# A decoder layer in split fp32 on one core: a gate stage's products put together, a reduction moved to the end of a queue, a pass's sums behind the next split, and more rooms for raw weights

## The chip, the cores and the metric

The kernel runs on one core of a Trainium2 chip. The time is device microseconds (us) of one execution; the kernel before was run three times, and the median of the three stands for it. TensorE (PE) does the matmuls, VectorE (DVE) and ScalarE (ACT) the work on elements, SyncE (SP) issues nearly all DMA loads. Each engine works through its instructions in the order of the program and stops at the first one whose inputs, or whose room, are not there yet.

## The reference

One decoder layer over 256 tokens of width 2048, all in fp32:

```python
h = rmsnorm(x, norm_mix_pre)
xr, yr, q, k, v, g_rnn, g_attn = split(h @ w_in)
xr = rg_lru(causal_depthwise_conv(xr), ...)      # block-diagonal gates: tanh/sigmoid of xb @ w_a, xb @ w_x
y_rnn = xr * gelu(yr)
y_att = sliding_window_sink_attention(rope(q), rope(k), v, sinks)
mix = sigmoid(g_rnn) * (y_rnn @ w_rnn_proj) + sigmoid(g_attn) * (y_att @ w_attn_proj)
x = x + rmsnorm(mix @ w_out, norm_mix_post)
u = square(relu(rmsnorm(x, norm_mlp_pre) @ w_mlp_up))
x = x + rmsnorm(u @ w_mlp_down, norm_mlp_post)
```

The up and down projections (2048 to 8192 and back) are over half of the weights that are read.

## The kernel before

**Products.** A number in fp32 is carried as two float32r parts, `hi` (the value cast down) and `lo` (what the cast left). A product of two such numbers is three matmuls: hi·hi, lo·hi, hi·lo. Weights arrive from memory as raw fp32 in halves of 128 x 1024 (512 KB). For each half ACT casts `whi` (L116), DVE subtracts to get `wlo` (L122), and PE uses both.

**The stream of weights.** The class `Stream` holds all weights in the order of their use. `load_to` issues SP's loads into the rooms `wraw` (four of them, `WRAW`), `split_to` emits cast and subtraction, `half` hands the next pair of parts to the matmul code and runs ahead: the split by six halves (`AHEAD`), the load by a few more. A load into a room waits until the subtraction that last read the room is done. There are six rooms each for `whi` and `wlo`. A second pool, tag `U8`, has 12 rooms of 128 x 2048 for activations and other large tiles.

**The recurrent stage.** `recur(m)` and `gates(m)` alternate for m = 0..3. `gates(m)` handles the two blocks n = 2m and 2m+1; each has two gates, and each gate is 12 matmuls of 128 x 256 into a bank `pg`, followed by two tanh on ACT (L799) that read the bank. For the odd block the two gates lie in the two banks of one pair tile. The matmuls that follow on PE belong to the next projection (`ps`, L264 with whi and L272 with wlo). Where nothing is pinned, a list scheduler with priorities sets the order on each engine; `fix` (keep_in_program_order) pins an instruction at its place.

**The residual.** After `w_out`, a generator `residual` is advanced step by step by `pump()`: for each half of the tokens (tb) and each quarter of the columns it forms the new x on DVE, squares it with a row sum on ACT, and writes x away. After the four quarters of a tb come a reduce, a root and a reciprocal (`rms`), and a diagonal matrix `dg`. `spread_r2` multiplies `ones` by both `dg` on PE (tile `pr`), which spreads the factor over all partitions; the first evacuations of the up projection need it. The pumps are spread over the opening of the up projection.

**Up and down.** The feed-forward work is done in two halves f = 0, 1: up (16 a-passes), then down in two passes n = 0, 1 of 1024 output columns each. A down pass goes over 16 pairs of weight halves. Seven of them (`SEVEN`: 0, 2, ..., 12) are done with seven products in place of eight (Strassen): DVE forms sums of the weights into a tile `t` (three operations), ACT and DVE split a, b and t (`whi`, `wlo`, `thi`, `tlo`), and PE runs 21 matmuls of 128 x 512. The other nine pairs are plain, 24 matmuls each. `t`, `thi` and `tlo` of each seven are U8 rooms. Eight banks are in use: four (`P1`, `P6` in s0, `Q5`, `N7` in s1) are complete after pair 12, four (`Q3`, `P2`, `Q4`, `Cs`) run to the end. After pair 12, DVE combines the first four into four tiles `t` (the sums; for f = 1 the earlier half's result `acc` is added too: eight DVE operations, `early`), and after the last matmul of each of the other banks, `finish` adds the bank to its tile. The last `held` pairs (2, and 3 in the very last pass) are done bank by bank, so that banks end one after another.

**Between the passes.** f = 0 writes its results to memory (`acc_away`); in f = 1 the generators `back` load them again, and in the last pass x1, the residual, as 256 KB pieces through SP, pumped between the pairs. The last pass also multiplies by a gain (`g3`), forms the row sums of squares, and ends with scale-and-add and the output's DMAs.

## Time and profile before

| | |
|---|---|
| three runs | 1540.43, 1539.72, 1537.09 us; median 1539.72 |
| the profiled execution | 1540.81 us; its span from first to last instruction 1539.0 us, so 1.8 us lie around it |
| PE busy | 1510.8 us, 98% of the span |
| DVE, ACT busy | 1108.1 us (72%), 826.4 us (54%) |
| granted PE clock, mean | 0.993 |
| HBM | 288.6 MB read, 192 GB/s over the span |

Times in the profile's rows are from the span's start. A row of a timeline has start, duration, engine, line, operation, out<-in, and in brackets how long the engine had been idle before and what released it. PEclk is the clock that PE was granted as a part of the full one, averaged over the stretch. The stages that matter here: recurrent stage with gates to about 585 us, up f0 from about 838, down f0 to 1174.7, up f1 to 1352.3, down f1 n0 to 1438.8, n1 to 1530.3, then the tail.

### The profile page before, as it was taken

The page shows a single profiled execution, that of the slowest core. Times are in us where ns is not written, and L with a number is a line of the kernel's source. Part 1 is how long each engine was busy: PE and PEld are TensorE (multiplying, and loading weights), DVE is VectorE, ACT ScalarE, POOL GpSimd, SP SyncE. Part 2 cuts the span into 40 slices and gives each one's busy share as a digit, 9 for nine tenths or more (in the row PEclk, how much of TensorE's full clock was granted, in tenths as well). Part 3 has the DMA queues.
Part 4 walks back from the last instruction along what each step waited for, and adds up shares of the span by engine and source line. Part 5 has one row for each costly group of instructions (what it writes and reads, how often), then busy time and mean ns, then how long its engine had stood idle before and what let it go on. Part 6 is the DMA issues. An engine that isn't in the chain of part 4 may idle for free.

```text
span 1539.0 us, 19994 instructions
## 1 busy us (share of the span) xinstructions
PE 1510.8 (98%) x7602; PEld 1267.5 (82%) x7602; DVE 1108.1 (72%) x1373; ACT 826.4 (54%) x1135; POOL 1.7 (0%) x9
## 2 busy tenths in 40 slices
PE   9999999999999999999999999999999999999996
PEld 7877778788888788888889888888888888888784
DVE  6676667857768867555667776689886666698877
ACT  6555555647566756444445555455454555555543
POOL 0000000000000000000000000000000000000000
PEclk9999999999999999999999999999999999999998
DMA  7645444364645565655865565656666655657574
GB/s 285 196 146 170 137 146 159 117 212 156 225 153 189 177 209 175 209 190 185 290 199 188 166 199 185 202 181 209 225 208 233 199 184 189 194 187 259 177 245 143
DMA packets 84191, 296.19 MB, mean 192 GB/s; under 512 B 9856, under 2 KB 10112, under 8 KB 83584
## 3 DMA queue, kind: packets, MB, share of 16 engines
q1 hardware_dynamic: 81072, 289.67, 57.6%
q10 hardware_dynamic: 3024, 5.25, 0.9%
q8 instruction: 59, 0.97, 0.3%
q14 instruction: 36, 0.29, 0.1%
HBM read 288.60 MB, written 6.29 MB: 192 GB/s over the span
## 4 chain that ended last, share of the span: by engine, by line
PE 83%; DVE 8%; DMA 5%; ACT 2%; issue 1%; SPq 0%; DVEq 0%; ACTq 0%
PE ps L931 20%; PE ps L264 6%; PE dQ L931 5%; DMA wraw<-in_w_dn 5%; DVE wlo L122 4%; PE ps L272 4%; PE dP L931 3%; PE s L931 2%; PE dCs L931 2%; PE gr L296 2%; PE gr L298 2%; PE pr L296 2%; PE pr L298 2%; PE pr L300 2%; PE pa L300 2%; PE pa L298 2%
## 5 line engine op out<-in xcount | busy, mean ns | idle before, releaser
L122 DVE TENSOR_TENSOR wlo<-wraw,whi 128x1024 fp32r<-128x1024 f32 x520 | 621.3, 1221 | 234.5 <-ACT whi L116 213.9
L116 ACT CAST whi<-wraw 128x1024 fp32r<-128x1024 f32 x520 | 533.5, 1050 | 461.3 <-DVE wraw L61 74.6
L931 PE MATMUL ps<-h2T,whi 128*128 128x512 f32 x976 | 228.8, 392 | 0.0
L931 PEld LDWEIGHTS ps<-h2T,whi 128*128 128x128 f32 x976 | 182.4, 189 | 36.9
L931 PEld LDWEIGHTS ps<-h2T,wlo 128*128 128x128 f32 x1024 | 127.0, 192 | 2.4
L931 PE MATMUL ps<-h2T,wlo 128*128 128x256 f32 x1024 | 127.9, 283 | 0.0
L264 PE MATMUL ps<-hT,whi 128*128 128x512 f32 x512 | 122.5, 395 | 0.0
L264 PEld LDWEIGHTS ps<-hT,whi 128*128 128x128 f32 x512 | 95.9, 190 | 20.5 <-issue 1.1
L931 PE MATMUL dQ<-whi,uT 128*128 128x512 f32 x288 | 107.8, 392 | 1.0 <-ACT whi L116 1.0
L272 PEld LDWEIGHTS ps<-hT,wlo 128*128 128x128 f32 x512 | 63.8, 191 | 1.8 <-issue 0.7
L272 PE MATMUL ps<-hT,wlo 128*128 128x256 f32 x512 | 65.2, 284 | 0.0
L931 PEld LDWEIGHTS dQ<-whi,uT 128*128 128x128 f32 x288 | 54.3, 189 | 13.1 <-ACT whi L116 2.2
L931 PE MATMUL dQ<-wlo,uT 128*128 128x512 f32 x144 | 57.0, 396 | 5.4 <-DVE wlo L122 5.4
L285 ACT COPY u<-ps 128x512 f32<-128x512 f32 x32 | 18.7, 585 | 80.2 <-PE ps L931 80.2
L61 DVE TENSOR_TENSOR t<-wraw,wraw 128x1024 f32<-128x1024 f32 x28 | 34.3, 1224 | 29.3 <-DMA wraw<-in_w_dn 28.1
L931 PE MATMUL dCs<-whi,uT 128*128 128x512 f32 x144 | 54.9, 398 | 0.0
L931 PE MATMUL dP<-whi,uT 128*128 128x512 f32 x144 | 53.8, 389 | 0.0
L296 PE MATMUL ga<-whi,hT 128*128 128x512 f32 x128 | 51.2, 400 | 0.0
L296 PE MATMUL q<-whi,hT 128*128 128x512 f32 x128 | 51.1, 399 | 0.0
L298 PE MATMUL ga<-wlo,hT 128*128 128x512 f32 x128 | 50.3, 393 | 0.0
L300 PE MATMUL ga<-whi,hT 128*128 128x512 f32 x128 | 50.2, 392 | 0.0
L298 PE MATMUL q<-wlo,hT 128*128 128x512 f32 x128 | 50.2, 392 | 0.0
(289 smaller groups left out, 2648.7 us busy)
## 6 DMA issues: line engine op xcount, KB each, us to landing
wraw<-in_w_dn SPq DMA_DIRECT2D x128, 512.0 KB, 5.0
wraw<-in_w_up SPq DMA_DIRECT2D x124, 512.0 KB, 5.0
wraw<-in_w_g SPq DMA_DIRECT2D x64, 512.0 KB, 4.7
wraw<-in_w_xy SPq DMA_DIRECT2D x64, 512.0 KB, 4.7
wraw<-in_w_q SPq DMA_DIRECT2D x32, 512.0 KB, 3.9
wraw<-in_w_ap SPq DMA_DIRECT2D x32, 512.0 KB, 4.7
wraw<-in_w_rp SPq DMA_DIRECT2D x32, 512.0 KB, 4.7
wraw<-in_w_out SPq DMA_DIRECT2D x32, 512.0 KB, 5.1
```

The source lines that it names most:

```text
L61: return lambda *args, **kw: self.pin(method(*args, **kw))
L116: self.pin(self.nc.scalar.copy(hi, src))
L122: self.last_low = self.pin(self.nc.vector.tensor_tensor(lo, src, hi.bitcast(F32), ALU.subtract))
L264: mm(ps[:, f].rearrange("p a b -> p (a b)"), hi[:, k * P : k * P + P], acts[kt // 4][:, kt % 4].rearrange("p a b -> p (a b)"), start=kt == ...
L272: mm(ps[:, f, 1, :], lo[:, k * P : k * P + P], acts[kt // 4][:, kt % 4, 0, :], start=False, stop=kt == KT - 1)
L285: ws.pin(nc.scalar.copy(out, ps[:, :, 1, :]))
L296: mm(banks[tb][n], a[:, 0, t], hi[:, n * 512 : n * 512 + 512], start=first, stop=False)
L298: mm(banks[tb][n], a[:, 0, t], lo[:, n * 512 : n * 512 + 512], start=False, stop=False)
L300: mm(banks[tb][n], a[:, 1, t], hi[:, n * 512 : n * 512 + 512], start=False, stop=last)
L931: return fix(mm(*args, **kw))
```

## The change

There are four parts.

**Gates.** The 24 matmuls of both gates of a block are written ahead of the four tanh, and pinned. In the program of before, the second gate of each odd block stood behind the beginning of the next projection. PE, third call of `gates` (n = 5); `whi_4214` is the gates' weight, `pg` the gates' bank, `ps` the next projection. Before:

```order
L796 MATMUL pg<-xs,wlo_4216 128x256
L264 MATMUL ps<-hT_121,whi_4268 128x512 x4
L264 MATMUL ps<-hT_122,whi_4268 128x512 x4
L264 MATMUL ps<-hT_123,whi_4282 128x512 x4
L264 MATMUL ps<-hT_124,whi_4282 128x512 x4
L264 MATMUL ps<-hT_121,whi_4306 128x512 x2
L794 MATMUL pg<-xs,whi_4214 128x256
```

The change:

```order
L198 MATMUL pg<-xs,whi_4214 128x256 x2
L198 MATMUL pg<-xs,wlo_4216 128x256
L271 MATMUL ps<-hT_121,whi_4268 128x512 x4
L271 MATMUL ps<-hT_122,whi_4268 128x512 x4
L271 MATMUL ps<-hT_123,whi_4282 128x512 x4
L271 MATMUL ps<-hT_124,whi_4282 128x512 x4
L271 MATMUL ps<-hT_121,whi_4306 128x512 x4
```

The last twelve `pg` matmuls now stand ahead of `ps`, which runs through in one piece.

**Residual.** Each square is emitted one pump later than the x that it reads, both `dg` come after all squares, and there is one pump more in the opening. DVE around the second `dg` (`st<-sqs` is the reduce over the squares, `wlo` the splits of the up projection's weights, `u<-ps` an evacuation). Before:

```order
L286 TENSOR_TENSOR u<-ps,u 128x512
L122 TENSOR_TENSOR wlo_7181<-wraw_7076,whi_7179 128x1024
L122 TENSOR_TENSOR wlo_7187<-wraw_7098,whi_7185 128x1024
L380 TENSOR_REDUCE st<-sqs 128x1
L382 RECIPROCAL st<-st 128x1
L61 TENSOR_SCALAR dg_7209<-ident,st 128x128
L122 TENSOR_TENSOR wlo_7240<-wraw_7112,whi_7238 128x1024
```

The change:

```order
L61 TENSOR_TENSOR og<-og,gp 128x512
L61 SCALAR_TENSOR_TENSOR x_6189<-og,st,x_6189 128x512
L293 TENSOR_TENSOR u<-ps,u 128x512
L122 TENSOR_TENSOR wlo_7176<-wraw_7077,whi_7174 128x1024
L122 TENSOR_TENSOR wlo_7182<-wraw_7094,whi_7180 128x1024
L387 TENSOR_REDUCE st<-sqs 128x1
L389 RECIPROCAL st<-st 128x1
L61 TENSOR_SCALAR dg_7204<-ident,st 128x128
L387 TENSOR_REDUCE st<-sqs 128x1
L389 RECIPROCAL st<-st 128x1
L61 TENSOR_SCALAR dg_7225<-ident,st 128x128
```

Both reductions now stand together behind the same two splits; the first one stood some fifteen operations earlier.

**Sums.** In all four down passes the sums are emitted after the splits of the pass's last pairs; in the two passes n0, where another down pass follows, DVE's list has them behind the split of that pass's first seven too. DVE at the end of down f1 n0 (`wlo_11927` and `wlo_11945` belong to pair 14, `wlo_11985` and `wlo_11989` to pair 15, `t_12007` to the next pass; `t<-s` and the rows up to `t<-t,acc` are the sums). Before:

```order
L122 TENSOR_TENSOR wlo_11927<-wraw_11863,whi_11925 128x1024
L122 TENSOR_TENSOR wlo_11945<-wraw_11878,whi_11943 128x1024
L61 TENSOR_TENSOR t<-s_11481,t 128x512
L61 TENSOR_TENSOR t<-s_11482,t 128x512
L61 TENSOR_TENSOR t<-t,s_11482 128x512 x2
L61 TENSOR_TENSOR t<-t,acc_11480 128x512
L61 TENSOR_TENSOR t<-t,acc_11479 128x512
L61 TENSOR_TENSOR t<-t,acc_11480 128x512
L61 TENSOR_TENSOR t<-t,acc_11479 128x512
L122 TENSOR_TENSOR wlo_11985<-wraw_11909,whi_11983 128x1024
L122 TENSOR_TENSOR wlo_11989<-wraw_11911,whi_11987 128x1024
L61 TENSOR_TENSOR t_12007<-wraw_11947,wraw_11929 128x1024
```

The change (`wlo_11968` and `wlo_11972` are pair 15 here):

```order
L122 TENSOR_TENSOR wlo_11941<-wraw_11799,whi_11939 128x1024
L122 TENSOR_TENSOR wlo_11968<-wraw_11830,whi_11966 128x1024
L122 TENSOR_TENSOR wlo_11972<-wraw_11830,whi_11970 128x1024
L61 TENSOR_TENSOR t_11989<-wraw_11875,wraw_11861 128x1024
L61 TENSOR_TENSOR wraw_11875<-t_11989,wraw_11861 128x512
L61 TENSOR_TENSOR t_11989<-wraw_11875 128x512
L122 TENSOR_TENSOR wlo_11997<-wraw_11861,whi_11995 128x1024
L122 TENSOR_TENSOR wlo_12001<-wraw_11875,whi_11999 128x1024
L61 TENSOR_TENSOR tlo_11991<-t_11989,thi_11990 128x1536
L61 TENSOR_TENSOR t<-s_11487,t 128x512
L61 TENSOR_TENSOR t<-s_11488,t 128x512
L61 TENSOR_TENSOR t<-t,s_11488 128x512 x2
```

The two splits of pair 15 and the six operations of the next pass's first seven now stand ahead of the sums.

**The last two passes.** In f = 1 the plain pairs (n0: 3, 5, ..., 15; n1: 1, 3, ..., 15) are loaded into one U8 room per pair, both halves, so that the four `wraw` rooms serve the sevens (in n0 also the pairs 1 and 14, in n1 pair 14); the load runs four halves further ahead where such pairs follow. `acc` and x1 come back in 512 KB pieces, x1 and the `spare` tile later than before. The gains for columns 0 to 1023 are loaded in the middle of the last pass, and their four multiplications of `acc` are put between its splits in place of its end. The last pass holds two pairs in place of three, and its final scale-and-adds are in another order: two of them go between the pieces of the root.

```diff
@@ class Stream, load_to
-            elif j < 2 * EXTRA:
+            elif j < 2 * EXTRA or j // 2 in self.wide:
                 if j % 2 == 0:
                     self.place = self.room(f"wraw{j}")
@@ ahead
-        self.load_to(max(2 * EXTRA, j + WHALF) + WRAW)
+        more = sum(i in self.wide for i in range(j // 2 + 1, (j + WHALF + WRAW) // 2 + 1))
+        self.load_to(max(2 * EXTRA, j + WHALF) + WRAW + (4 if more > 1 else 0))
@@ layer
+            if f == 1:
+                apart.update(len(chunks) + i for i in range(1 if n else 3, PAIRS, 2))
@@ gates
             if n % 2:
-                second = pair_banks("pg")
-            for gate, g in enumerate((ga, gx)):
-                pg = second[gate][0] if n % 2 else bank(psg, "pg")
+                pgs = [b[0] for b in pair_banks("pg")]
+            else:
+                pgs = [bank(psg, "pg") for gate in range(2)]
+            for gate, pg in enumerate(pgs):
                 ...
-                        mm(dst, hi[:, c], xs[:, k, 0, :], start=k == 0, stop=False)
+                        ordered(dst, hi[:, c], xs[:, k, 0, :], start=k == 0, stop=False)
                 ...
+            for gate, g in enumerate((ga, gx)):
+                pg = pgs[gate]
                 for f in range(2):
@@ residual
                 v.scalar_tensor_tensor(x1[:, tb, c], og[:, tb, c], r1[tb], x1[:, tb, c], ALU.mult, ALU.add)
+                yield
                 sc.activation(og[:, tb, c], x1[:, tb, c], AF.Square, accum_out=sq[:, 2, tb, q : q + 1])
                 sc.dma_start(x1_away[tb][:, c], x1[:, tb, c])
-                yield
+        for tb in range(TB):
+            yield
             dg = pb.tile([P, P], F32, name=f"dg{tb}")
@@ the opening of up
-        if i in (2, 4):
+        if i in (1, 2, 4):
             pump()
@@ down: the block "if p == SEVEN[-1]" is taken out, and stands here
         parts = [[ws.half(False) for i in range(2)] for p in range(held)]
+        for name in ((1, 0), (0, 0), (1, 1), (0, 1)):
+            ready[name] = u2("t")
+        x = ready[0, 0]
+        sc.copy(ready[1, 0], banks["P1"])
+        v.tensor_tensor(x, banks["P6"], ready[1, 0], ALU.add)
+        ...
+        early(ready)
         ws.split_to(ws.at + 2)
@@ f = 1
+        def back_x1():
+            g = [u2("g") for k in range(2)]
+            for k in range(2):
+                fix(nc.sync.dma_start(g[k], gains[3][quarter(k)].partition_broadcast(P)))
+            yield
+            for tb in range(TB):
+                for k in range(2):
+                    yield
+                    c = quarter(k)
+                    v.tensor_tensor(acc[tb][:, c], acc[tb][:, c], g[k], ALU.mult)
+            for tb in range(TB):
+                x1.append(flat(unit(f"x1{tb}", F32)))
+                yield from back(x1[tb], x1_away[tb])
@@ finish, last pass
-            r = rms(tb, 3)
-            for q in range(4):
-                ...
+            if i == 1:
+                r, root = [st[:, 12 + 2 * tb + k : 13 + 2 * tb + k] for k in range(2)]
+                v.tensor_reduce(r, sq[:, 3, tb, :], AX.X, ALU.add)
+                sc.activation(root, r, AF.Sqrt, bias=eps, scale=1.0 / D)
+                if tb:
+                    away_with(0, 3)
+                v.reciprocal(r, root)
+                r3.append(r)
+            for q in [(), (0,), (1, 2), (0, 1, 2, 3)][2 * tb + i]:
+                away_with(tb if i else 0, q)
@@
-        down(f, n, uT, 3, [(0, 0), (0, 1), (1, 0), (1, 1)], finish, early)
+        down(f, n, uT, 2, [(0, 0), (0, 1), (1, 0), (1, 1)], finish, early)
```

## The prediction, on record before the run

> **What bounds the kernel now.** I read the page's busy times and its chain of waits first, then PE's waits by what released them, then a table of stretches.

> ```profile
> PE 1510.8 (98%) x7602; PEld 1267.5 (82%) x7602; DVE 1108.1 (72%) x1373; ACT 826.4 (54%) x1135; POOL 1.7 (0%) x9
> PE 83%; DVE 8%; DMA 5%; ACT 2%; issue 1%; SPq 0%; DVEq 0%; ACTq 0%
> ```

> PE is the bound: 28 us of the span are not PE's, and 83% of the chain is PE's own work. The change does not take a matmul away, so it can gain only what PE loses by waiting and by a lower clock. PE's waits:

> ```profile
> PE dQ L931 <- DVE wlo L122: 5.4, 5, 3.2
> PE pg L794 <- ACT room L799: 3.7, 1, 3.7
> PE pr L931 <- DVE dg L61: 2.5, 1, 2.5
> PE s L931 <- DVE wlo L122: 1.5, 1, 1.5
> PE dQ L931 <- ACT whi L116: 1.0, 1, 1.0
> ```

> These five rows (us in total, times, longest) are 14.1 us, and each is a place that the change touches. The stretches around them, then the down passes f0 n1, f1 n0, f1 n1:

> ```profile
> core 0: us, PE busy (x) PEld busy (x) DVE busy (x) ACT busy (x) POOL busy (x), PEclk, DMA share, GB/s
> 503.00:513.00 10.00, 6.28 (x22) 5.41 (x22) 7.21 (x11) 8.92 (x17) 0.00 (x0) 0.66 0.47 147
> 860.00:870.00 10.00, 7.46 (x32) 6.06 (x31) 8.12 (x14) 5.90 (x10) 0.00 (x0) 0.83 0.63 205
> 1421.00:1432.00 11.00, 7.63 (x32) 5.66 (x31) 10.44 (x14) 3.96 (x5) 0.00 (x0) 1.00 0.53 188
> 1511.00:1521.00 10.00, 7.82 (x21) 5.38 (x21) 8.10 (x12) 1.61 (x3) 0.00 (x0) 0.66 0.32 104
> 1092.50:1174.70 82.20, 82.20 (x364) 68.08 (x363) 67.52 (x64) 41.01 (x39) 0.00 (x0) 1.00 0.68 225
> 1352.30:1438.80 86.50, 83.13 (x367) 68.20 (x366) 74.94 (x74) 44.01 (x46) 0.00 (x0) 1.00 0.69 225
> 1438.80:1530.30 91.50, 87.04 (x364) 69.14 (x362) 75.10 (x79) 42.25 (x48) 0.00 (x0) 0.96 0.61 196
> ```

> A down pass without a stall is 82.2 us: 7·21 + 9·24 = 363 matmuls at 0.227 us, so a seven takes 4.76 us and a plain pair 5.44. The last two passes take 4.3 and 9.3 us more. A granted clock of 0.66 over 10 us is 3.4 us of clock lost, 0.83 is 1.7 us.

> **Gates.** ACT and PE at the third call:

> ```profile
> 498.89 4.26 PE L264 MATMUL ps<-hT,whi 128*128 128x512 f32 x18
> 506.87 0.58 PE L794 MATMUL pg<-xs,whi 128*128 128x256 f32 x1 [3.72 <-ACT room L799]
> 506.01 0.81 ACT L799 ACTIVATE room<-pg,bh 128x256 f32<-128x256 f32 x2
> 509.84 0.84 ACT L799 ACTIVATE room<-pg,bh 128x256 f32<-128x256 f32 x2 [1.05 <-PE pg L796]
> 513.57 2.93 ACT L116 CAST whi<-wraw 128x1024 fp32r<-128x1024 f32 x3
> ```

> The second gate's matmuls stand behind 18 of the next projection and wait for the first gate's tanh, since both gates share one tile. PE idles 3.72 us and then runs at the lower clock: 3.4 us less about 0.4 that fell into the idle time leaves 3.0. Written ahead of the tanh, the matmuls wait for nothing, so up to 6.7 us go. What is late next is the casts at 513.57, which feed the projection after this one. PE will reach it near 511.2: 498.9, 1.4 for the twelve gate matmuls of half width, 7.3 and 3.6 for the 32 wide and 32 half-wide ones of `ps`. Of what stands ahead of the casts on ACT, only the idle gap of 1.05 us goes, so they start near 512.5. The first of that projection's halves is cast already and lasts PE 1.8 us, to 513.0; the second comes at 513.5. That is 0.5 us of new waiting, so −6.2; bounds −6.7 (none) and −4.0 (2.7 us, if the casts stay where they are and the later halves wait too). The three other calls did not stall and give nothing.

> **Residual.** PE waits for the second `dg`:

> ```profile
> 863.77 0.49 PE L931 MATMUL pr<-dg,ones 128*128 128x128 f32 x2 [2.54 <-DVE dg L61]
> 852.53 0.63 ACT L61 ACTIVATE og<-x 128x512 f32<-128x512 f32 x1 [2.74 <-DVE x L61]
> 860.44 2.36 DVE L122 TENSOR_TENSOR wlo<-wraw,whi 128x1024 fp32r<-128x1024 f32 x2 [0.25 <-ACT whi L116]
> 862.72 0.15 DVE L380 TENSOR_REDUCE st<-sqs 128x1 f32<-128x4 f32 x1
> ```

> The reduce stands behind two splits that wait for casts, and on ACT a square that waits for its x (2.74 us at 852.53) holds the casts behind it; one such stop comes ahead of each square. With the squares one pump later the x is there, and by my count down both queues the casts come some 4 us earlier: the two splits end near 858.7, where they ended at 862.7. Two reductions follow in place of one, each about 1.0 us to its `dg` (862.72 to 863.77), so the second is done at 860.7, and PE arrives there 2.93 us ahead of 863.77, at 860.84. I price the stall with its clock: 2.54 + about 1.6 (0.17 of 10 us) = 4.2. Bounds: −4.2 if it goes whole, −2.5 if 1.2 us of waiting stay and 0.5 of clock. I take −4.0, since the count leaves 0.1 us. [...] The rows differ: 2.54 us was followed by a clock of 0.83, and 3.20 us (next part) by 1.00. [...]

> **Sums, f1 n0.** DVE between pairs 14 and 15, and PE behind it:

> ```profile
> 1422.50 1.48 DVE L61 TENSOR_TENSOR t<-s,t 128x512 f32<-128x512 f32 x2
> 1427.62 2.35 DVE L122 TENSOR_TENSOR wlo<-wraw,whi 128x1024 fp32r<-128x1024 f32 x2
> 1428.89 0.50 PE L931 MATMUL dQ<-wlo,uT 128*128 128x512 f32 x1 [3.20 <-DVE wlo L122]
> ```

> The sums, 1422.50 to 1427.6, keep pair 15's splits 5.1 us from PE; this is the 3.2 us wait and nearly all of the pass's 4.3. In the new order pair 15 is split by about 1422.3, the next seven by 1428.9 (it costs 6.6, below), the sums end at 1434.0, the first `finish` at 1434.7. The next pass, now due at 1434.5, wants that bank 0.7 us after its start. So nothing waits, with 0.5 us to spare; bounds −4.3 and −3.2, I take −4.2.

> **The same move, f0 n0.** Here before lost nothing, so the move can only cost:

> ```profile
> 1083.67 1.23 DVE L61 TENSOR_TENSOR t<-wraw,wraw 128x1024 f32<-128x1024 f32 x1 [0.88 <-DMA wraw<-in_w_dn]
> 1090.21 0.68 DVE L61 TENSOR_TENSOR t<-dQ,t 128x512 f32<-128x512 f32 x1
> 1093.13 0.39 PE L931 MATMUL dQ<-whi,seven 128*128 128x512 f32 x1
> 1093.82 2.95 ACT L116 CAST whi<-wraw 128x1024 fp32r<-128x1024 f32 x3 [5.59 <-DVE t L61]
> ```

> The seven's split (1083.67 to 1090.21, 6.5 us) starts with a DMA and stays where it is. The sums (four operations, 2.76 us) now follow it, to 1093.0; the first `finish` ends at 1093.65, and PE wants its bank at 1093.13: 0.5 us. ACT's casts at 1093.82 stand behind `finish` and move by about 2 us, which costs pair 1 up to 0.4 more. +0.8; bounds 0, and +4.2 if this wait drops the clock as the one of 2.54 did. At the end of f0 n1 the next work is an up pass, whose banks are others: nothing.

> **Last pass.** DVE's groups in f1 n1, and the two places where the lead breaks:

> ```profile
> L122 DVE TENSOR_TENSOR wlo<-wraw,whi 128x1024 fp32r<-128x1024 f32 x30 | 35.5, 1219 | 5.1 <-ACT whi L116 4.9
> L61 DVE TENSOR_TENSOR tlo<-t,thi 128x1536 fp32r<-128x1536 f32 x6 | 10.5, 1750 | 0.0
> L61 DVE TENSOR_TENSOR t<-wraw,wraw 128x1024 f32<-128x1024 f32 x6 | 7.3, 1224 | 9.9 <-DMA wraw<-in_w_dn 8.7 <-PE s L931 1.2
> L61 DVE TENSOR_TENSOR acc<-acc,g 128x512 f32<-128x512 f32 x4 | 2.6, 683 | 0.0
> 1448.69 5.01 DMA wraw<-in_w_dn
> 1498.05 1.23 DVE L61 TENSOR_TENSOR t<-wraw,wraw 128x1024 f32<-128x1024 f32 x1 [3.58 <-DMA wraw<-in_w_dn]
> 1501.91 0.50 PE L931 MATMUL s<-wlo,seven 128*128 128x512 f32 x1 [1.51 <-DVE wlo L122]
> ```

> A seven and a plain pair cost DVE 6.6 + 2.4 = 9.0 us against PE's 10.2, so DVE has time. But a seven's raw halves can be loaded only into rooms that the seven before has just freed (the chain's row: 5.0 us for the load), so DVE's loop is 5.0 + 5.0, about PE's 10.2, with no slack for a late load; one came 3.58 us late, and the lead was gone. The rest of the pass lost 4.5 us in waits of dQ and s, and the clock (0.66 at the end, 3.4 less what fell into idle time). With four rooms for the sevens alone, a load has two periods, and DVE is bound by itself: 9.0 + 0.7 (one multiplication of `acc` in four of the periods) of 10.2. The lead at the start is thin, since the first plain pair's casts stand behind four squares: 0.5 to 1 us by my count, growing 0.5 to 1.2 us with each period. The wide loads and the `tlo` of each seven wait for PE to leave older U8 rooms; that gives `tlo` 8.4 us (a plain pair and the first 2.95 us of a seven) for 1.75 us of work, and the wide loads some 20 us. Bounds: −9.3 (all of it), −4.5 (waits as many as now, without the clock). I take −8.4, nearer the first, as every row of loss in this pass goes back to the raw weights.

> **Tail.** Behind the last matmul one scale-and-add stands between reduce and reciprocal:

> ```profile
> 1532.42 0.17 DVE L382 RECIPROCAL st<-st 128x1 f32<-128x1 f32 x1 [0.36 <-ACT st L381]
> 1532.62 1.41 DVE L61 SCALAR_TENSOR_TENSOR x<-acc,st,x 128x512 f32<-128x512 f32 x2
> ```

> It takes 0.7 us where 0.36 were idle: +0.4. Holding two pairs in place of three gives `finish` 2.72 us a bank, which its three or four operations of 0.7 us fill. Bounds 0 and +0.6.

> **The sum.** −6.2 − 4.0 − 4.2 − 8.4 + 0.8 + 0.4 = −21.6; 1540.81 − 21.6 = 1519.2. The profiled execution is 1.1 us over the median of the runs, which span 3.3 us; I write 1519.0 for a median. All at their best ends give −24.5, so 1516.3, and 1.1 to 3.7 less against the other runs: the likeliest case has its own range, 1514 to 1524.

> **The rivals.** *The last pass stays bound by its feeding*: the U8 rooms that the wide loads need are freed by PE, the lead stays thin, and the 9.3 us stay. For it: the wait of `t` on PE (1.2 us in the row above). Against it: the 20 us and 8.4 us of room. Time 1519 + 8.4 = 1527.4. *The sums hold the banks*: at one or both n0 ends the finish is late enough to stop PE for about 2.5 us and the clock with it; one costs 4.2, both 8.4: 1523 to 1527. For it: spare times of 0.5 and −0.5 us. *The gates' stall moves* to the next projection's casts, so the part does not do what it says: about 1525; for it the casts at 513.57, against it the gaps on ACT. *Slower*: SP's queue is in order, and a wide load at its head that waits for PE holds the sevens' raw halves behind it. If each such hold is like the one at 1498.05 (3.58 on DVE, 1.51 on PE, and 1.7 of clock, 3.2 in all), the first two parts' 10.2 us are used up by four of the twelve later sevens, beside the 13.6 us of the two passes that would then stay; with all twelve it is +38.4 − 10.2, about 1569. Against it: the wide loads wait for pairs that PE leaves some 20 us before they are wanted.

> [...]

> **How the numbers follow.** Forecast 0.63; last pass bound 0.13; sums hold the banks 0.09; gates' stall moves 0.06; slower 0.05; parts that undo each other near no change 0.04. A difference of 0.2%, 3.1 us, is about what a measurement of this kernel can tell. Faster: the first four, 0.91, less 0.01 for mixtures; within 0.2%: 0.04; slower 0.06. The range 1514 to 1530 holds the forecast and the three middle cases but for their edges, a good 8 in 10.

> **What would show it.** In the profile after: no `pg` row among PE's waits and a clock of 1.00 around 503; `pr` waits under 1 us; PE's span of f1 n0 82 to 83 us, with `t<-s` behind `tlo` on DVE; in f1 n1 no DMA wait of `t` that matters, a clock of 1.00, and a pass of 82 to 84 us; a wait of `dQ` or `dP` of about 0.5 us at the start of f0 n1. Wrong would be: a wait of `ps` on casts after the gates over 2 us, a wait on DVE at a pass's first matmuls over 2 us, or `t` waiting for DMA or PE in f1.

## The result, and the profile after

The changed kernel takes 1517.92 us (median of four runs, 1517.25 to 1518.49); the kernel before 1540.03 (four runs, 1537.09 to 1540.43). The ratio is 0.986 with a 95% interval of 0.9843 to 0.9877: 1.4% faster, 22.1 us. The prediction was 1519.0, in a range from 1514 to 1530.

The profiled execution took 1517.25 us, with a span of 1515.4. The page's busy times and chain, and then PE's waits (what waits, for what: us in total, times, longest):

```profile
PE 1501.4 (99%) x7602; PEld 1263.9 (83%) x7602; DVE 1107.3 (73%) x1373; ACT 825.4 (54%) x1135; POOL 1.7 (0%) x9
PE 89%; DVE 5%; DMA 3%; ACT 1%; issue 1%; SPq 0%; DVEq 0%; ACTq 0%
```

```profile
PE pt L690 <- DVE s L681: 1.2, 4, 0.4
PE kv L397 <- DVE ones L359: 1.1, 1, 1.1
PE kv L460 <- ACT whi L116: 0.8, 2, 0.4
PE front L418 <- DMA x<-in_x: 0.5, 1, 0.5
PE dQ L198 <- DVE t L61: 0.4, 1, 0.4
```

All five rows that carried the prediction's argument are gone. One row is new: dQ for t, 0.4 us. Where half-clock stretches stood before, and in the down passes f0 n1, f1 n0 and f1 n1, the table of stretches (us of the stretch, busy time of each engine, then PEclk, DMA share, GB/s):

```profile
495.00:505.00 10.00, 10.00 (x66) 9.10 (x65) 8.39 (x12) 8.49 (x16) 0.00 (x0) 1.00 0.64 197
848.00:858.00 10.00, 10.00 (x63) 9.01 (x62) 7.80 (x14) 5.87 (x10) 0.00 (x0) 1.00 0.63 202
1080.30:1163.60 83.30, 82.86 (x365) 67.98 (x364) 69.80 (x68) 40.91 (x39) 0.00 (x0) 1.00 0.68 224
1341.40:1423.70 82.30, 82.30 (x366) 68.13 (x365) 74.73 (x74) 42.68 (x44) 0.00 (x0) 1.00 0.78 262
1423.70:1506.10 82.40, 82.40 (x364) 67.92 (x362) 74.27 (x79) 42.61 (x50) 0.00 (x0) 1.00 0.55 182
```

The clock is full in all of them, and both passes of f = 1 are at the 82.2 us of a pass without a stall, to 0.2 us. Only f0 n1 is longer than it was, by 1.1. From the starts of the same matmuls in the two timelines comes the ledger, which adds up to the 23.6 us between the two spans:

| stretch | predicted | measured |
|---|---|---|
| ahead of the gates, and from there to the residual | 0 | −1.0 |
| third gates call | −6.2 | −6.7 |
| residual, `dg` | −4.0 | −4.4 |
| f0 n0 to n1 | +0.8 | +1.0 |
| f1 n0 | −4.2 | −4.0 |
| last pass | −8.4 | −9.1 |
| tail | +0.4 | +0.6 |

### The profile page after: what moved, and what is told of

Read it like the earlier page. It is cut to its first block, busy times and chain, and to the rows that moved or that the text cites. A ratio compares the mean times of both kernels' runs of the same rounds, so it can differ in the third digit from the quotient of the medians.

```text
span 1515.4 us, 19989 instructions
## 1 busy us (share of the span) xinstructions
PE 1501.4 (99%) x7602; PEld 1263.9 (83%) x7602; DVE 1107.3 (73%) x1373; ACT 825.4 (54%) x1135; POOL 1.7 (0%) x9
## 4 chain that ended last, share of the span: by engine, by line
PE 89%; DVE 5%; DMA 3%; ACT 1%; issue 1%; SPq 0%; DVEq 0%; ACTq 0%
PE ps L198 22%; PE ps L271 7%; PE dQ L198 7%; PE s L198 4%; PE ps L279 4%; PE dP L198 3%; PE dCs L198 2%; DMA wraw<-in_w_dn 2%; PE gr L305 2%; PE pa L305 2%; PE gr L303 2%; PE pr L303 2%; PE pr L307 2%; PE pa L307 2%; PE pr L305 2%; PE q L303 2%
## 5 line engine op out<-in xcount | busy, mean ns | idle before, releaser
L122 DVE TENSOR_TENSOR wlo<-wraw,whi 128x1024 fp32r<-128x1024 f32 x520 | 621.9, 1220 | 228.5 <-ACT whi L116 212.5
L116 ACT CAST whi<-wraw 128x1024 fp32r<-128x1024 f32 x520 | 533.2, 1050 | 435.4 <-DVE wraw L61 64.1
L61 DVE TENSOR_TENSOR tlo<-t,thi 128x1536 fp32r<-128x1536 f32 x28 | 49.0, 1751 | 2.7 <-ACT thi L140 2.7
```

Of the source, the lines that this page charges most:

```text
L61: return lambda *args, **kw: self.pin(method(*args, **kw))
L116: self.pin(self.nc.scalar.copy(hi, src))
L122: self.last_low = self.pin(self.nc.vector.tensor_tensor(lo, src, hi.bitcast(F32), ALU.subtract))
```

## The experiments

Times are medians, each beside runs of the kernel before on the same chip. In them the kernel before gave medians of 1539.6 to 1540.3 us.

**The gates' part alone, on the kernel before** (the 24 matmuls pinned, then the tanh).

```diff
-            for gate, g in enumerate((ga, gx)):
-                pg = second[gate][0] if n % 2 else bank(psg, "pg")
+            for gate, pg in enumerate(pgs):
```

> The kernel before with the gates' part of the change alone. Theory (each part removes a stall of its own place, and the gains add): PE's wait of pg for the tanh (3.72 us) and the half clock behind it go, 6.7 us by the two profiles' marks, so 1540.0 - 6.7 = 1533.3 us; the clock around the third gates call is 1.00, all other stalls stay. Rival (the clock's drop moves on: what falls at one stall is owed to the phase of something else): the wait goes, but a low clock of some 3 to 7 us shows elsewhere, so 1535 to 1537.

Measured: 1534.52 us (1532.6 to 1537.91; ratio 0.9962, interval 0.9948 to 0.9977), 5.7 us less. The wait of pg is gone and no new one stands near. But the gap at the end of f1 n0, 3.20 us before and followed by a clock of 1.00, was now followed by 0.83. The timelines have 2.94 us of waiting there, and these are the stretches behind the waits for `dg` and at that gap:

```profile
853.00:863.00 10.00, 7.47 (x31) 6.06 (x30) 8.26 (x14) 5.52 (x9) 0.00 (x0) 0.83 0.62 208
1420.00:1430.00 10.00, 8.01 (x27) 6.21 (x28) 9.93 (x12) 2.48 (x3) 0.00 (x0) 0.83 0.50 156
```

So the stall went whole, as the theory says, and the rival's point, a low clock that turns up elsewhere, was seen once too. The 1.0 us between 5.7 and 6.7 is of that size: by the starts of the matmuls, the old gates cost 6.7 us in the first profile of before, but 6.6, 5.8 and 5.4 us in the three other profiles that have them.

**The residual's part alone, on the kernel before.**

```diff
                 v.scalar_tensor_tensor(x1[:, tb, c], og[:, tb, c], r1[tb], x1[:, tb, c], ALU.mult, ALU.add)
+                yield
                 sc.activation(og[:, tb, c], x1[:, tb, c], AF.Square, accum_out=sq[:, 2, tb, q : q + 1])
-                yield
+        for tb in range(TB):
+            yield
             dg = pb.tile([P, P], F32, name=f"dg{tb}")
-        if i in (2, 4):
+        if i in (1, 2, 4):
```

> The kernel before with the residual's part alone (squares a pump later, both dg at the end, one pump more). Theory: PE's wait for the second dg (2.54 us) and its clock go, 4.4 us by the marks: 1535.6 us, second dg ready 0.1 us before PE wants it. Rival (a wait of 2.54 us costs only itself, the clock falls for another reason): 1537.5, and a half-clock stretch still near 864.

Measured: 1535.9 us (1533.86 to 1537.23; ratio 0.9965, interval 0.9953 to 0.9978), 4.35 us less. PE does not wait for `dg`, and the gain is 1.8 us more than the wait of 2.54 us that it had: the theory, with the clock in the price.

**The sums' part alone, on the kernel before** (the copy and the four operations of `sums`, with `early(ready)`, move).

```diff
-                if p == SEVEN[-1]:
-                    ...
         parts = [[ws.half(False) for i in range(2)] for p in range(held)]
+        ...
```

> The kernel before with the sums' move alone, in all four down passes; four rooms for raw weights as before. Theory (the sums ahead of pair 15's splits are the whole of the 4.0 us of down f1 n0): that pass goes to 82.5 us, f0 n0's end costs 1.0 us, the last pass stays near 91.5: 1540.0 - 4.0 + 1.0 = 1537.0 us. Rival (raw weights for pairs 14 and 15 are late anyway, and without more rooms the splits stay late): n0 keeps 2 to 4 us of its loss, 1539 to 1541 us, with splits of pair 15 waiting for casts that wait for DMA.

Measured: 1543.26 us (1538.13 to 1546.07; ratio 1.0016, interval 1.0004 to 1.0028): 3.0 us slower than before. The theory holds for f1 n0, and both were blind to what came next. The profile is of the second fastest of the ten executions (1540.54 us), so it shows where time was lost, not the whole of the 3.0 us. Stretches of f1 n0 and of the last pass:

```profile
1351.80:1434.30 82.50, 82.50 (x364) 68.03 (x364) 69.45 (x65) 42.28 (x41) 0.00 (x0) 1.00 0.71 233
1434.30:1529.20 94.90, 87.70 (x364) 69.44 (x362) 79.44 (x88) 43.79 (x52) 0.00 (x0) 0.96 0.58 190
```

The last pass gives back 3.4 us, at its first bank. DVE's and PE's timelines there:

```profile
1426.37 1.23 DVE L61 TENSOR_TENSOR t<-wraw,wraw 128x1024 f32<-128x1024 f32 x1 [0.84 <-DMA wraw<-in_w_dn]
...
1432.90 1.41 DVE L61 TENSOR_TENSOR t<-s,t 128x512 f32<-128x512 f32 x2
...
1437.95 0.68 DVE L61 TENSOR_TENSOR acc<-dQ,t 128x512 f32<-128x512 f32 x1
```

```profile
1438.69 0.50 PE L931 MATMUL dQ<-whi,seven 128*128 128x512 f32 x1 [3.53 <-DVE acc L61]
```

Read it upward: PE wants the bank that `finish` frees; `finish` stands behind the sums; the sums stand behind the next pass's first seven; and the seven starts when its raw weights land, at 1426.37. This is the rival "the sums hold the banks", in a kernel with four rooms.

**The change without the rooms.**

```diff
-            if f == 1:
-                apart.update(len(chunks) + i for i in range(1 if n else 3, PAIRS, 2))
```

> The changed kernel without the U8 rooms for plain pairs in f = 1: all raw halves share the four rooms again; sums, gains, late x1, two held pairs stay as changed. Theory (the rooms are what ends the last pass's loss): the sevens wait for DMA again, the last pass is 88 to 92 us in place of 82.3, and f1 n0 may lose 1 to 3: 1517.9 + 6 to 12 = 1524 to 1530 us. Rival (the multiplications of acc taken from the end, x1 loaded later and two held pairs did it): the last pass stays under 84 us, 1518 to 1520 us.

Measured: 1531.58 us (1526.76 to 1533.46; ratio 0.9934, interval 0.9912 to 0.9956), 13.7 us over the changed kernel by the medians and a little more than the theory's band. The edit also takes back the load's running four halves further ahead, which hangs on the rooms. Its profile is of the fastest of the four executions: f1 n0 83.6 us, the last pass 89.1, and the tail 12.5 where the changed kernel has 9.7. DVE's group of the sevens' first sums in the last pass, without the rooms and, in the second fence, in the changed kernel (busy, mean ns, then the idle time ahead and what ended it):

```profile
L61 DVE TENSOR_TENSOR t<-wraw,wraw 128x1024 f32<-128x1024 f32 x6 | 7.3, 1224 | 6.6 <-DMA wraw<-in_w_dn 6.4
```

```profile
L61 DVE TENSOR_TENSOR t<-wraw,wraw 128x1024 f32<-128x1024 f32 x6 | 7.3, 1216 | 0.0
```

The rooms, with the longer run ahead, are the part that ends the waits for raw weights; the gains' new place, the late loads of x1 and two held pairs do not do it alone.

**The sums of f1 n0 back behind pair 12, in the changed kernel.**

```diff
+                if p == SEVEN[-1] and (f == 1 and n == 0):
+                    sums_now()
```

> The changed kernel with the sums of down f1 n0 alone back behind pair 12, ahead of pair 15's splits; rooms and all else as changed. Theory A (with weights in their rooms early, pair 14's splits are done before pair 12 ends, so the sums start at once, about 1407.6 to 1412.7, and pair 15's first split is there at 1413.9, when PE wants it at 1414.2): the pass stays at 82.3 to 82.8 us, 1517.9 + 0 to 0.5 = 1518 us; the move is then needed only without the rooms. Theory B (the prediction's: the sums' place is what cost 4.0 us there): the wait of dQ for wlo of 3 us returns, 1522 us.

Measured: 1517.5 us (1516.75 to 1518.45; ratio 0.9858, interval 0.9842 to 0.9875). The wait does not return, and f1 n0 is 82.3 us without a gap on PE:

```profile
1340.80:1423.10 82.30, 82.30 (x365) 68.18 (x364) 74.86 (x74) 43.76 (x47) 0.00 (x0) 1.00 0.78 262
```

Theory A.

**The rooms in the last pass only.**

```diff
-            if f == 1:
-                apart.update(len(chunks) + i for i in range(1 if n else 3, PAIRS, 2))
+            if f == 1 and n:
+                apart.update(len(chunks) + i for i in range(1, PAIRS, 2))
```

> The changed kernel with the U8 rooms for plain pairs in the very last pass only, not in f1 n0. Theory (in the run without any such rooms, f1 n0 lost 1.2 us and the last pass's first matmuls waited 2.7 us for a finish, since the seven behind which the sums stand got its weights late): n0 83 to 84 us and a wait of dQ for acc of 1 to 3 us at the start of the last pass, then no further loss: 1517.9 + 1.5 to 5 = 1519.5 to 1523 us. Rival (only the last pass's own loads matter): 1518 us.

Measured: 1528.05 us (1524.44 to 1528.8; ratio 0.992, interval 0.9905 to 0.9935), worse than the theory's band, mostly in the way it says: in the profile f1 n0 takes 84.6 us, and the last pass 7.7 us more than in the changed kernel, which is the wait below and the clock behind it. Another 1.5 us over the changed kernel lie in f0 n1, half of them at its first bank. DVE's timeline at the end of f1 n0, PE's behind it, and the stretch:

```profile
1419.85 1.23 DVE L61 TENSOR_TENSOR t<-wraw,wraw 128x1024 f32<-128x1024 f32 x1 [2.98 <-DMA wraw<-in_w_dn]
1431.44 0.68 DVE L61 TENSOR_TENSOR acc<-dQ,t 128x512 f32<-128x512 f32 x1
```

```profile
1432.18 0.80 PE L198 MATMUL dQ<-whi,seven 128*128 128x512 f32 x1 [4.09 <-DVE acc L61]
```

```profile
1427.00:1437.00 10.00, 5.79 (x14) 4.29 (x15) 8.16 (x14) 4.84 (x11) 0.00 (x0) 0.70 0.12 46
```

A seven that waits 2.98 us for its weights becomes 4.09 us of PE's and a clock of 0.70. In the run without any rooms the seven itself waited 0.23 us, but a split ahead of it had waited 2.40 us for its cast, and the cast for its weights; PE's wait was 2.67.

**The sums of both f = 0 passes back behind pair 12, and the tail in plain order.**

```diff
+                if p == SEVEN[-1] and (f == 0):
+                    sums_now()
-                if tb:
-                    away_with(0, 3)
                 v.reciprocal(r, root)
```

> The changed kernel with the sums of both f = 0 passes back behind pair 12, and the last scale-and-adds in plain order (none between reduce and reciprocal). Theory (the two places where the prediction had a cost, by the profiles 1.0 us at f0 n0's end and 0.6 us in the tail): 1517.9 - 0.5 to 1.6 = 1516.3 to 1517.4 us, no wait of dQ for t. Rival (the wait of 0.4 us at f0 n0 comes from late weights and varies from run to run, and the tail's 0.6 us are not the order's): 1517.9 us, no difference that five rounds tell.

Measured: 1516.96 us (1516.51 to 1517.44; ratio 0.9853, interval 0.9838 to 0.9867). The wait of dQ for t is gone and f0 n1 starts without loss. The tail is not better: from the last matmul's start to the span's end it takes 10.0 us, against 9.7 to 9.8 in the seven profiles that have the change's order and its rooms in the last pass. With all four scale-and-adds ahead, the last `finish` starts 0.7 us later after that matmul, so the order of the change is the better one for two held pairs.

**The third pump kept, squares and dg in the old order.**

```diff
-                yield
                 sc.activation(og[:, tb, c], x1[:, tb, c], AF.Square, accum_out=sq[:, 2, tb, q : q + 1])
                 sc.dma_start(x1_away[tb][:, c], x1[:, tb, c])
+                yield
-        for tb in range(TB):
-            yield
```

> The changed kernel with the residual's squares and dg in the old order, but with the third pump kept. Theory (the squares that stop ACT until their x is there hold the casts; a pump more shifts only one quarter): part of the wait comes back, PE waits 1 to 2 us for dg, 1519 to 1521 us. Rival (the added pump alone brings the second dg early enough): no wait, 1518 us.

Measured: 1520.06 us, one run. The rival is right on the wait: there is none for `dg`. DVE and PE around it:

```profile
848.40 1.23 DVE L122 TENSOR_TENSOR wlo<-wraw,whi 128x1024 fp32r<-128x1024 f32 x1 [1.73 <-ACT whi L116]
851.80 0.16 DVE L387 TENSOR_REDUCE st<-sqs 128x1 f32<-128x4 f32 x1 [0.79 <-ACT og L61]
852.52 0.29 DVE L61 TENSOR_SCALAR dg<-ident,st 128x128 f32<-128x128 f32 x1
```

```profile
854.33 0.60 PE L198 MATMUL pr<-dg,ones 128*128 128x128 f32 x4
```

The pump puts the second reduction ahead of the two splits that it stood behind, and `dg` is there 1.5 us before PE. ACT still stops for squares (the cast 1.73 us late), and PE pays for that in other rows, 0.6 us for u and 0.4 us for whi; f0 n0's end cost 1.9 us in this run. By the starts of the matmuls, this profile loses 0.6 us more than the changed kernel's behind the gates, 1.5 at the residual and 0.9 at f0 n0's end. The time lies in the theory's band, though the wait that it named is not there; which of these losses is the edit's, a single run does not settle.

**Late sums in the last pass only.**

```diff
+                if p == SEVEN[-1] and (f == 0 or n == 0):
+                    sums_now()
```

> The changed kernel with the sums back behind pair 12 in three of the four down passes; only the last pass keeps them late. Theory A (with the rooms, the sums' move gains nothing in f1 n0, and in f0 n0 it costs 0 to 1.9 us by when the next seven's weights land): f0 n0's end costs nothing, f1 n0 82.3 us, 1517.9 - 0.4 to 1.2 = 1516.7 to 1517.5 us. Theory B (late sums pay somewhere): 1518 to 1520 us.

Measured: 1516.34 us (1515.82 to 1516.86; ratio 0.9841, interval 0.9826 to 0.9855).

**The change without its sums part.**

```diff
+                if p == SEVEN[-1]:
+                    sums_now()
```

> The changed kernel without its sums part: sums behind pair 12 in all four passes, rooms, gains, late x1 and two held pairs as changed. Theory A: in the last pass, too, pair 15's first split is there in time (sums 5.1 us after pair 12, splits 2.4, the first wanted 6.8 us after pair 12): at most 0.8 us of wait, 1516.5 to 1518.3 us. Theory B (the sums stall pair 15 in the last pass as they did in f1 n0 before): 1520 us and more, with a wait of dQ for wlo.

Measured: 1516.48 us (1516.42 to 1517.01; ratio 0.9842, interval 0.9828 to 0.9857). Theory A in both, the first 0.4 us under its band. In the last pass of the kernel before, the sums stood behind all splits already; this run puts them ahead of pair 15's there, and it costs nothing either. The stretches of f1 n0 and of the last pass, and DVE in f1 n0, without the sums part:

```profile
1341.00:1423.30 82.30, 82.30 (x365) 68.19 (x364) 74.93 (x74) 43.76 (x47) 0.00 (x0) 1.00 0.77 262
1423.30:1505.70 82.40, 82.40 (x364) 67.97 (x363) 73.81 (x78) 41.47 (x46) 0.00 (x0) 1.00 0.55 182
```

```profile
1399.99 4.83 DVE L122 TENSOR_TENSOR wlo<-wraw,whi 128x1024 fp32r<-128x1024 f32 x4
1407.22 0.69 DVE L61 TENSOR_TENSOR t<-s,t 128x512 f32<-128x512 f32 x1 [0.73 <-PE s L198]
1409.15 2.49 DVE L61 TENSOR_TENSOR t<-t,acc 128x512 f32<-128x512 f32 x4
1411.56 2.35 DVE L122 TENSOR_TENSOR wlo<-wraw,whi 128x1024 fp32r<-128x1024 f32 x2
1423.54 0.69 DVE L61 TENSOR_TENSOR acc<-dCs,t 128x512 f32<-128x512 f32 x1 [1.30 <-PE dCs L198]
```

The splits of pair 14 are done early enough that DVE waits for PE to end pair 12 (0.73 us), and those of pair 15 follow at 1411.56. Before, with four rooms, pair 14's splits waited for ACT's casts, these for DMA, and the sums began only behind them, at 1422.50. ACT's two casts of pair 14 and DVE's two splits, before:

```profile
1417.56 1.05 ACT L116 CAST whi<-wraw 128x1024 fp32r<-128x1024 f32 x1 [1.88 <-DMA wraw<-in_w_dn]
1420.27 1.05 ACT L116 CAST whi<-wraw 128x1024 fp32r<-128x1024 f32 x1 [1.66 <-DMA wraw<-in_w_dn]
1418.64 1.23 DVE L122 TENSOR_TENSOR wlo<-wraw,whi 128x1024 fp32r<-128x1024 f32 x1 [0.52 <-ACT whi L116]
1421.36 1.23 DVE L122 TENSOR_TENSOR wlo<-wraw,whi 128x1024 fp32r<-128x1024 f32 x1 [1.49 <-ACT whi L116]
```

Both versions without late sums in f = 0 lie 1.4 to 1.6 us under the changed kernel by medians (1517.92 us, and 1517.79 in four more executions of the same program, next). Their eight times go from 1515.82 to 1517.01, the changed kernel's eight from 1516.4 to 1518.94. Only one of the changed kernel's lies within the others' range, but the intervals of the ratios overlap, so I call it likely, with the 1.0 us of f0 n0 as its place.

**x1's rooms and the spare room taken early.**

```diff
-        x1 = []
+        x1 = [flat(unit(f"x1{tb}", F32)) for tb in range(TB)]
-        spare, r3 = [], []
+        spare, r3 = [flat(unit("spare", F32))], []
```

> The changed kernel with x1's two rooms and the spare room taken from the U8 rooms at the start of the last pass, as before; their loads stay where the change has them. Ten of the twelve U8 rooms are then held through the pass, and t, thi, tlo and the wide loads share two. Theory (it is the late x1 that makes the rooms for the wide loads): sevens wait for PE to leave rooms, DVE's t waits for PE, the last pass 88 us or more, 1524 us or more. Rival (two rooms turn over fast enough): 1518 us.

Measured: 1517.79 us (1516.4 to 1518.94; ratio 0.9853, interval 0.9835 to 0.987). The edit did not do what it was meant to: the program that comes of it is the changed kernel's, instruction for instruction, with `x1` and `spare` in the same U8 rooms. In the trace the loads of the last pass are issued at the same times after its start, to 0.1 us. A seven needs three rooms at once (`t`, `thi`, `tlo`), so two free ones could not have served it. The run is thus four more executions of the changed kernel and decides nothing between theory and rival; what the late loads of x1 are worth was not tested. It does show that naming the two tiles later, which the change also does, has no effect by itself.

**The kernel before, once more.**

> The kernel before, once more, for its clock. Theory (whether a wait of about 3 us brings the half clock depends on where it falls against windows of 3.41 us that run on by themselves): the same waits of 3.7, 2.5 and 3.2 us, but the half-clock stretches may sit at another choice of them, each a multiple of 3.41 us; time 1537 to 1543 us. Rival (the length of the wait or the work around it decides): half clock again after the 3.7 and 2.5 us waits and not after that of 3.2.

Measured: 1539.99 us. PE waits 3.95, 2.54 and 3.00 us at the same three places. The stretches behind them:

```profile
502.00:512.00 10.00, 6.05 (x25) 5.02 (x25) 7.78 (x12) 9.74 (x19) 0.00 (x0) 0.83 0.49 157
858.00:868.00 10.00, 7.46 (x33) 6.10 (x32) 8.12 (x14) 5.89 (x10) 0.00 (x0) 0.83 0.62 205
1425.00:1435.00 10.00, 7.96 (x27) 6.11 (x28) 9.93 (x11) 2.43 (x2) 0.00 (x0) 0.83 0.50 162
```

The same kernel, the same waits to 0.3 us, and another clock: the first place has 0.83 where it had 0.66, the third 0.83 where it had 1.00. That is the theory's side, and the rival, by which the same waits bring the same clock, falls; where the stretches lie in time is in the last section.

## Why the prediction was right, and where not

**PE's waits as the whole of what could be gained** held: the matmuls are the same 7602, and all but the tail's 0.6 us of the ledger are waits and clock of PE. The prediction's sum was −21.6, the ledger's is −23.6. The terms were read from one profile of before and are measured against the same one, so part of their fit is that execution's: in the three other profiles with the old order in f1 n0 and the last pass, f1 n0 lost 4.3 to 5.4 us where this one lost 4.0, and the last pass 7.6 to 9.0 where it lost 9.1.

**Gates**, −6.2 of a possible −6.7: 6.7 went. The 0.5 us of new waiting did not come. The casts on ACT after the change:

```profile
504.43 1.04 ACT L116 CAST whi<-wraw 128x1024 fp32r<-128x1024 f32 x1
510.20 0.63 ACT L825 ACTIVATE room<-room 128x512 f32<-128x512 f32 x1
511.26 1.03 ACT L116 CAST whi<-wraw 128x1024 fp32r<-128x1024 f32 x1
512.20 0.63 ACT L825 ACTIVATE room<-room 128x512 f32<-128x512 f32 x1
```

I had counted the casts behind both roots (L825), as before. The scheduler put one cast between them, and that cast came at 511.26 where I had 512.5 (about 511.9 on this profile's scale, which runs 0.6 us earlier here). The projection starts at 510.84 and has a half in hand. I had the three other calls at nothing; the fourth gave 0.26 us (last item). The rival "the gates' stall moves" did not come about: PE runs through into that projection without a wait.

**Residual**, −4.0: 4.4, with the count of the queues right to 0.1 us (second `dg` done 852.95, PE there at 853.08; I had 860.7 and 860.84 on the old scale). The cause that I named was too narrow. I gave the gain to the squares that stop ACT; the third pump alone removes the wait for `dg`, by another way (it puts the reduction ahead of the splits). The run that keeps only the pump shows that; what the squares' new place adds is not settled. The price with the clock was right: the one run that isolates it gave 4.35 us, at least 3.4 by its interval, against the 2.54 us of the wait without the clock.

**Sums in f1 n0**, −4.2: the pass gained 4.0, and this step named the cause wrongly all the same. In the kernel before, the sums did stand in the way, and moving them alone makes the pass 82.5 us. But with the rooms the pass takes 82.3 us without the move too, so in the changed kernel the move is worth nothing there. What made the sums stand in the way was late raw weights: pair 14's splits came late, so the sums did, and so pair 15's splits. I took the place in the list for the cause and did not ask what the list would look like once the weights were early. The two terms, −4.2 and −8.4, are one: without the rooms the change is 13.7 us slower, more than both together, and without the move nothing is missing. That the sum came out all the same is luck in this step: the rooms paid for both terms.

**Sums in f0 n0**, +0.8: 1.0 in the profile, by the mechanism as put: the first `finish` ends late and PE waits 0.44 us for it, and pair 1 pays the rest. Across the runs that move these sums, the end of f0 n0 cost 0 (three times), 1.0, 1.2, 1.8 and 1.9 us; the start of the next seven, which its weights set, decides it. In these seven profiles PE waited for nothing where the seven started over 10 us ahead of the next pass, 0.4 to 0.6 us where it was 8.7 to 8.8, and 1.2 to 1.4 us where it was 7.9 to 8.1. Without the whole sums part the changed kernel is likely 1.4 us faster, so the part costs and gains nothing.

**Last pass**, −8.4: 9.1. Nearly all of it went, and the thin lead at the start held. The rival for U8 rooms, "stays bound by its feeding", falls by the profile: no `t` of the last pass waits for DMA or for PE. So does "slower": of SP's waits in the last two passes, 0.7 us are for PE, and no seven's weights are late behind them. The 1.7 us of clock that it counted for each hold were my estimate from another place, a row with 0.83, and no run shows them for such a hold: around the one at 1498.05 the profile of before has a clock of 1.00 over 1498 to 1508 us. The rival "the sums hold the banks" did not come about in the changed kernel, where the first `finish` had 1.4 us to spare (done at 1422.92, wanted at 1424.36; I had 0.5); it is real where f1 n0 has four rooms, 3.5 us in one run, 2.7 and 4.1 in two others. The condition that I left out of it is where the seven's weights are.

**Tail**, +0.4: 0.6, but much of that is the draw of one execution. From the last matmul's start to the end the old order took 9.1, 9.1, 9.6, 9.7 and 9.8 us in five profiles, the new one 9.7 to 9.8 in seven. The old order's long ones have the last `finish` later, behind other work. The rows of `finish` in the first and in the second profile of before (last matmul at 1529.93 and 1528.60), and in the changed kernel (1505.73):

```profile
1530.36 0.69 DVE L61 TENSOR_TENSOR acc<-dQ,t 128x512 f32<-128x512 f32 x1 [0.17 <-PE dQ L931]
1529.56 0.68 DVE L61 TENSOR_TENSOR acc<-dQ,t 128x512 f32<-128x512 f32 x1
1506.24 0.68 DVE L61 TENSOR_TENSOR acc<-dQ,t 128x512 f32<-128x512 f32 x1
```

The order of the scale-and-adds is not the price; the plain order took 0.3 us more. Against the first profile, 0.1 us comes from that `finish`, 0.2 from the reciprocal, and the rest from the landing of the last outputs and the end behind it, whose cause is open.

**What no step had**: 1.0 us. PE's wait of kv for its first casts was 2.0 us in the profile of before, 0.7 to 1.6 us in ten others and nothing in three, among them the second profile of the same kernel; the 0.4 us that the profile of before is late by at 15 us are the one execution. Another 0.26 us lies at the fourth call of `gates`: all four profiles with the old gates have it, none with the new ones, so it belongs to the gates' part. The rest is 0.2 us or less at a place.

## What to carry to other kernels

When an instruction stands in another's way in an in-order queue, ask first why it reached the head so late: here one cure (weights in earlier) made the other (a new order) needless, and alone the new order was slower by 3 us. Make sure that an edit reaches the program, too: one of these experiments changed a line and nothing else. A move behind work that starts with a DMA can inherit the DMA's lateness (2.98 us of it became 4.09 us of PE's in one run); price it with the weights late, not as they landed in one profile. And a sum of parts that each fit is no proof of their causes: undo each part in the finished kernel, too, and drop the one that is worth nothing; here that is the sums, and the versions near 1516.4 us are likely the better ones.

## What the runs showed of the chip

The low clock did not follow the length of a wait alone. Waits of 2.54 us for `dg` were followed by 0.83 over 10 us in both profiles of the kernel before. At the end of f1 n0, 3.20 us were followed by 1.00 (the first profile of before), 3.00 us by 0.83 (the same kernel again) and 2.94 us by 0.83 (the gates' part alone). At the last pass's first bank, 2.67 us were followed by 1.00 in the run without rooms, and 4.09 us by 0.70 with the rooms in the last pass only.
